# A two-layer decoder trunk on one core: the up projections' matmuls sorted by width, and low parts moved 64 bytes

## The chip, the cores and the metric

The kernel runs on one core of a Trainium2 chip. The metric is the device time of one execution in microseconds (us); three runs of the kernel before have a median of 771.84 (771.66 to 772.72). TensorE (PE) multiplies, VectorE (DVE) and ScalarE (ACT) do elementwise work, GpSimd (POOL) a few small steps, and SyncE's queue (SP) issues the transfers from main memory (HBM) to the on-chip memory (SBUF). Matmul results land in PSUM. A matmul has a *stationary* operand, which a weight load (LDWEIGHTS, PEld in the profile) brings into the array, and a *moving* one, which streams past it, one column of the result per column of the operand.

## The reference

The input x is 256 tokens by 1024 features, float32. Layer 0 mixes tokens by dilated attention (three patterns, 16 heads of 64), layer 1 by forgetting attention; a dense feed-forward layer follows each, and a final norm ends it.

```python
def swiglu(h, w_gu, w_down):
    gu = h @ w_gu
    g, u = gu[..., :D_FF], gu[..., D_FF:]
    return (jax.nn.silu(g) * u) @ w_down

for i in range(DEPTH):                         # DEPTH = 2
    h = h + mixer[i](rmsnorm(h, norm[i]))      # projections, attention, output projection
    h = h + swiglu(rmsnorm(h, ffn_norm[i]), ffn_w_gu[i], ffn_w_down[i])   # D_FF = 2816
return rmsnorm(h, final_norm)
```

All inputs are float32, and every weight is read once from HBM.

## The kernel before

**Three-part products.** A float32 matrix is split into a high part, rounded to the format `float32r` that TensorE streams in one pass, and a low part, the remainder. `split` (L73, L74) does this: ScalarE copies into the high tile, VectorE subtracts it from the source into the low tile. A product is then the sum of high x high, high x low and low x high, three matmuls into one PSUM bank: `mm3` (L172, L173, L174).

**Weights.** `piece` fetches a weight piece of 128 x 2048 in two halves into `raw` tiles (5 buffers of 4 KB per partition) and splits each half into `wh` and `wl` (4 buffers of 8 KB each). `weights` keeps two pieces ahead in a fixed order of pieces.

**x^T.** `xt_tile` holds the normalised activations transposed: for each of 8 depths k (128 features each) 256 columns of the high part and behind them 256 of the low part, in one tile of 16 KB per partition with one buffer. It is used by every projection of a mixer and of a feed-forward layer.

**Projections.** `proj_feat` takes weights as stationary operand and x^T as moving one (256 columns, feature-major result); `proj_tok` and `proj_pair` take x^T as stationary operand and weights as moving one (256 and 512 columns, token-major result). `out_proj` and `down` take attention outputs (`oth`, `otl`) or activations (`ah`, `al`) as stationary operand and 512 columns of weights as moving one.

**The up projection, `proj_wide`.** For 19 of the 22 pieces of each feed-forward layer, once for the gate and once for the up half, it goes through the 8 depths. At each depth one matmul (L224) has the high weights stationary and streams high and low of x^T together, 512 columns into the whole bank; the next (L225) has the low weights stationary and streams the high part, 256 columns into the bank's first half. Widths thus alternate 512, 256, 512, 256. Behind it ScalarE and VectorE add the bank's halves, and apply the gate. The first three pieces of each feed-forward layer (its head) run through `proj_tok` instead, while the second half of the tokens is still being normalised.

**What sets the order.** All of it is written in program order, and a planner places each engine's instructions by that order and by a priority (`first()` lifts the few that shorten a chain). The last up projection of each feed-forward layer is lifted whole, so it interleaves with the one before it.

**Where tiles lie.** Three pools stand one behind the other in SBUF: `cst`, `wp` (weights) and `ap` (all else). In a pool, the first use of a name reserves all its buffers at the next free address, each rounded up to 32 bytes. `p_tile` gives a tile of 768 floats, which serves attention weights and, with 512 floats used, the high and low activations `ah` and `al` of the feed-forward layers. A tile of 112 floats (448 bytes) that nothing reads stands ahead of x^T. Small tiles for norms and softmax (`rs`, `ssq`, `nm`, `den`, `gates`, `rs_a`, `rt`) lie where their first use comes.

Of the kernel before, what the change touches and what calls it, by code (L numbers as in the profile page):

```python
# [10 lines left out]
F32 = mybir.dt.float32  # L11
F32R = mybir.dt.float32r
# [4 lines left out]
P = 128  # L17
D = 1024
S = 256
KT = D // P  # L20
NH = 16
# [10 lines left out]
def trunk(ctx: ExitStack, tc: tile.TileContext, T, out):  # L32
    nc = tc.nc

    cst = ctx.enter_context(tc.tile_pool(name="cst", bufs=1))
    wp = ctx.enter_context(tc.tile_pool(name="wp", bufs=1))
    ap = ctx.enter_context(tc.tile_pool(name="ap", bufs=1))
    ps = ctx.enter_context(tc.tile_pool(name="ps", bufs=1, space=bass.MemoryType.PSUM))

    ALL = slice(None)  # L40
# [8 lines left out]
    def hrow(name):  # L49
        return ap.tile([P, D], F32, tag="h", name=name, bufs=4)  # L50
# [16 lines left out]
    euler = cst.tile([P, 1], F32, name="euler")  # L67
    nc.gpsimd.memset(euler, math.e)

    def split(pair, view, src, early=True):  # L70
        hi, lo = pair
        with first() if early else nullcontext():
            return (nc.scalar.activation(view(hi), src, AF.Copy),  # L73
                    nc.vector.tensor_tensor(view(lo), src, view(hi).bitcast(F32), op=ALU.subtract))  # L74
# [18 lines left out]
    def fm_tile(tag, n, bufs):  # L93
        return tuple(ap.tile([P, n, S], F32R, tag=f"{tag}{x}", name=f"{tag}{x}", bufs=bufs) for x in "hl")
# [1 line left out]
    class XT(tuple):  # L96
        pass

    def xt_tile():
        full = ap.tile([P, KT, 2, S], F32R, tag="xt", name="xt", bufs=1)  # L100
        x = XT((full[:, :, 0, :], full[:, :, 1, :]))
        x.full = full
        return x
# [72 lines left out]
    def both(pair, *idx):  # L176
        return tuple(x[idx] for x in pair)
# [41 lines left out]

    def proj_wide(xt, w, o, c):  # L220

        for k in range(KT):
            wh, wl = both(w, ALL, slice(k * 256 + c * P, k * 256 + (c + 1) * P))
            nc.tensor.matmul(o.rearrange("p (x s) -> p x s", x=2), wh, xt.full[:, k], start=k == 0, stop=False)  # L224
            nc.tensor.matmul(o[:, :S], wl, xt[0][:, k], start=False, stop=k == KT - 1)  # L225


    def p_tile(n=512, dtype=F32, name="p"):
        return ap.tile([P, 768], dtype, tag="p", name=name, bufs=6)[:, :n]

    def v_tile(o=None, r=None):

# [57 lines left out]
    o = psum("o")  # L290
    for n in (256, 256, 256, 256, 128):
        nc.tensor.matmul(o[:, :n], mhalf.to_broadcast([P, P]), mhalf.to_broadcast([P, n]), start=True, stop=True)
    with tc.high_priority(offset=1000):
# [1 line left out]

    room = [hrow("xw0"), hrow("xw1"), *(y.rearrange("p k c -> p (k c)").bitcast(F32) for y in fm_tile("ot", KT, 1)),
            wp.tile([P, 2048], F32, tag="wh", name="xw4", bufs=4)]
    xk, wk, xs = [], [], []  # L300
    for i, c in enumerate(room):
        b = 1 + (i > 1)
        n = S + 512
# [12 lines left out]
        for j in range(b):  # L316
            xk.append(both_k[:, j, :S])
            wk.append(both_k[:, j, S:])

    ap.tile([P, 112], F32, tag="gap", name="gap", bufs=1)  # L320
    xt = xt_tile()

    r_a = []
    lead = [psum("sc") for _ in range(2)]
# [49 lines left out]
    with first(), in_order(cut):  # L374
        a = square(4)
# [11 lines left out]
    def rstd_a():  # L387

        o = psum("tr")
        for t in range(2):  # L390
            nc.tensor.matmul(o[:, t:t + 1], part[0][:, t * P:(t + 1) * P], one, start=True, stop=True)
        v = ap.tile([P, 4], F32, tag="rs_a", name="rs_a", bufs=1)
        with first():
            nc.scalar.activation(v[:, :2], o[:, :2], AF.Copy, bias=EPS)
            nc.gpsimd.tensor_tensor(v[:, 2:], v[:, :2], mhalf.to_broadcast([P, 2]), op=ALU.pow)
        r_a.extend(v[:, 2 + t:3 + t] for t in range(2))

    x = []
# [101 lines left out]
    for i, (hq, g, w) in enumerate(a_units):  # L500
# [18 lines left out]
        if w < 2:  # L519
# [4 lines left out]
            if i == 2:  # L524
                values_12(quad["v"], lead)

                wt = weights("a_in", 1)
                o_next = psum("mm")
                rb = psum("tr")

                def rows():
                    for t in range(2):
                        nc.tensor.matmul(rb[:, t * P:(t + 1) * P], r_a[t].to_broadcast([P, P]), ident,
                                         start=True, stop=True)

                proj_feat(xt, wt, o_next[:, :S], 0, (6, rows))
                for c in (rcos, rsin):
                    nc.vector.tensor_tensor(c, c, rb[:, :S], op=ALU.mult)
                rt = ap.tile([P, 2], F32, tag="rt", name="rt", bufs=1)
                tmp = ap.tile([P, D], F32, tag="xn", name="rd", bufs=2)[:, :S].rearrange("p (b c) -> p b c", b=2)  # L540
                e = early(rb[:, :S], None)
                nc.vector.tensor_tensor(tmp, e, ident[:, None, :].to_broadcast([P, 2, P]), op=ALU.mult)
                nc.vector.tensor_reduce(rt, tmp, axis=AX.X, op=ALU.add)
# [65 lines left out]
    def out_proj(nm, ot, h, grow, done, banks):  # L609

        ws = [weights(nm, i) for i in range(4)]
        xt = xt_tile()
        res = []

        def part(t, acc, nk):
# [36 lines left out]
    def ffn(l, hs, xt, grow, mid):  # L652
        acc = {}
        acts = {}

        def act(f):
            if f % 2 == 0:
                acts[f // 2] = tuple(p_tile(512, F32R, f"a{y}") for y in "hl")
            return acts[f // 2], lambda y: y[:, (f % 2) * S:(f % 2 + 1) * S]

        def gated(g, u, shape):
# [94 lines left out]

    def mid(h0):
        nxt["g"] = load_grow(2)
        nxt["xt"] = xt_tile()
        norm_t(*h0, nxt["g"], nxt["xt"], 0)  # L760

    hs = ffn(0, hs, xt, g_f, mid)
# [6 lines left out]
    split((wf[:, :, :NH], wf[:, :, 32:32 + NH]), lambda y: y, wf32.rearrange("p (k c) -> p k c", k=KT))  # L769

    gt = v_tile()
    ga = ap.tile([P, 6, 2 * NH], F32, tag="gates", name="gates", bufs=1)


    own = (slice(0, 64), slice(64, 128))
# [286 lines left out]
```

## Time and profile before

| | |
|---|---|
| median of 3 runs | 771.84 us (771.66 to 772.72) |
| the profiled execution's own time | 772.96 us |
| its span | 771.1 us |
| granted TensorE clock, mean | 0.996 of full |
| PE busy | 760.3 us (99%) |
| weight loads busy | 675.2 us (88%) |
| DVE busy | 535.7 us (69%) |
| ACT busy | 429.9 us (56%) |
| HBM read | 133.05 MB, 174 GB/s over the span |

A row of the groups reads: line, engine, operation, out<-in by the program's names, partitions x columns, count | busy us, mean ns of one | idle time of the engine just before them, and what ended it. For a matmul, `128*128 128x512` is a stationary operand of 128 x 128 and a moving one of 128 x 512. Matmuls are pipelined: their recorded durations overlap, so the time that one costs in a stream is the difference between its start and the next one's. A timeline row begins with the start and the duration in us.

### The profile page before, as it was taken

The page shows a single profiled execution, that of the slowest core. Times are in us where ns is not written, and L with a number is a line of the kernel's source. Part 1 is how long each engine was busy: PE and PEld are TensorE (multiplying, and loading weights), DVE is VectorE, ACT ScalarE, POOL GpSimd, SP SyncE. Part 2 cuts the span into 40 slices and gives each one's busy share as a digit, 9 for nine tenths or more (in the row PEclk, how much of TensorE's full clock was granted, in tenths as well). Part 3 has the DMA queues.
Part 4 walks back from the last instruction along what each step waited for, and adds up shares of the span by engine and source line. Part 5 has one row for each costly group of instructions (what it writes and reads, how often), then busy time and mean ns, then how long its engine had stood idle before and what let it go on. Part 6 is the DMA issues. An engine that isn't in the chain of part 4 may idle for free.

```text
span 771.1 us, 12961 instructions
## 1 busy us (share of the span) xinstructions
PE 760.3 (99%) x5152; PEld 675.2 (88%) x5152; DVE 535.7 (69%) x834; ACT 429.9 (56%) x740; POOL 33.4 (4%) x51
## 2 busy tenths in 40 slices
PE   9999999999999999999999999999999999999996
PEld 7988999999998798888888888999889888888885
DVE  7897986976988476665566474887756656567644
ACT  7735628448538455545565464586655455556532
POOL 1110000010010000000000003110000000000000
PEclk9999999999999999999999999999999999999999
DMA  9864561752663367555567544643326655656601
GB/s 330 291 198 158 164 213 63 236 176 88 206 215 118 98 217 242 185 192 190 180 199 232 153 148 153 217 139 122 119 89 228 214 195 183 192 190 196 213 1 54
DMA packets 38348, 134.93 MB, mean 175 GB/s; under 512 B 4368, under 2 KB 5648, under 8 KB 38288
## 3 DMA queue, kind: packets, MB, share of 16 engines
q1 hardware_dynamic: 38144, 134.01, 52.6%
q8 instruction: 40, 0.66, 0.3%
q14 instruction: 20, 0.16, 0.1%
q10 hardware_dynamic: 144, 0.10, 0.0%
HBM read 133.05 MB, written 1.05 MB: 174 GB/s over the span
## 4 chain that ended last, share of the span: by engine, by line
PE 86%; DVE 5%; ACT 3%; DMA 2%; issue 2%; POOL 1%; SPq 0%; POOLq 0%; DVEq 0%; ACTq 0%
PE ps_mm L172 10%; PE ps_mm L174 10%; PE ps_mm L173 10%; PE ps_tr L224 9%; PE ps_mm L224 9%; PE ps_mm L225 5%; PE ps_tr L225 5%; PE ps_sc L174 4%; PE ps_sc L172 4%; PE ps_sc L173 4%; PE ps_o L174 3%; PE ps_o L173 3%; PE ps_o L172 3%; PE ps_tr L272 2%; PE ps_o L283 2%
## 5 line engine op out<-in xcount | busy, mean ns | idle before, releaser
L74 DVE TENSOR_TENSOR wl<-raw,wh 128x1024 fp32r<-128x1024 f32 x236 | 284.0, 1219 | 146.3 <-ACT wh L73 146.0
L73 ACT ACTIVATE wh<-raw 128x1024 fp32r<-128x1024 f32 x236 | 243.7, 1056 | 154.2 <-PE ps_tr L224 34.8
L172 PE MATMUL ps_mm<-xt,wh 128*128 128x256 f32 x512 | 144.1, 281 | 0.0
L174 PE MATMUL ps_mm<-xt,wl 128*128 128x256 f32 x512 | 142.3, 278 | 0.1
L173 PE MATMUL ps_mm<-xt,wh 128*128 128x256 f32 x512 | 142.1, 278 | 0.0
L224 PE MATMUL ps_tr<-xt,wh 128*128 128x512 f32 x304 | 108.8, 397 | 0.0
L224 PE MATMUL ps_mm<-xt,wh 128*128 128x512 f32 x304 | 108.7, 397 | 0.0
L174 PEld LDWEIGHTS ps_mm<-xt,wl 128*128 128x128 f32 x512 | 96.5, 188 | 0.5 <-DVE wl L74 0.5
L172 PEld LDWEIGHTS ps_mm<-xt,wh 128*128 128x128 f32 x512 | 96.2, 188 | 0.4
L173 PEld LDWEIGHTS ps_mm<-xt,wh 128*128 128x128 f32 x512 | 96.4, 188 | 0.2
L225 PE MATMUL ps_mm<-xt,wl 128*128 128x256 f32 x304 | 85.1, 281 | 0.0
L225 PE MATMUL ps_tr<-xt,wl 128*128 128x256 f32 x304 | 85.1, 281 | 0.0
L224 PEld LDWEIGHTS ps_tr<-xt,wh 128*128 128x128 f32 x304 | 57.0, 188 | 13.9
L224 PEld LDWEIGHTS ps_mm<-xt,wh 128*128 128x128 f32 x304 | 57.0, 188 | 13.6
L172 PE MATMUL ps_mm<-wh,xt 128*128 128x256 f32 (+1 forms) x176 | 60.2, 342 | 2.0 <-DVE fm L409 2.0
L173 PE MATMUL ps_mm<-wl,xt 128*128 128x256 f32 (+1 forms) x176 | 59.1, 336 | 0.0
L174 PE MATMUL ps_mm<-wh,xt 128*128 128x256 f32 (+1 forms) x176 | 59.0, 336 | 0.0
L225 PEld LDWEIGHTS ps_mm<-xt,wl 128*128 128x128 f32 x304 | 57.1, 188 | 0.9
L225 PEld LDWEIGHTS ps_tr<-xt,wl 128*128 128x128 f32 x304 | 57.1, 188 | 0.2
L73 ACT ACTIVATE ah<-sa 128x256 fp32r<-128x256 f32 x38 | 15.9, 418 | 49.5 <-DVE sa L684 49.5
L172 PEld LDWEIGHTS ps_mm<-wh,xt 128*128 128x128 f32 x176 | 33.9, 193 | 6.1 <-issue 2.4
L174 PEld LDWEIGHTS ps_mm<-wh,xt 128*128 128x128 f32 x176 | 33.8, 192 | 3.7 <-DVE xt L74 0.3
(243 smaller groups left out, 1263.3 us busy)
## 6 DMA issues: line engine op xcount, KB each, us to landing
raw<-in_gu SPq DMA_DIRECT2D x88, 512.0 KB, 4.7
raw<-in_a_in SPq DMA_DIRECT2D x68, 512.0 KB, 4.6
raw<-in_dn SPq DMA_DIRECT2D x44, 512.0 KB, 4.7
raw<-in_b_in SPq DMA_DIRECT2D x24, 512.0 KB, 4.9
raw<-in_a_out SPq DMA_DIRECT2D x8, 512.0 KB, 4.0
raw<-in_b_out SPq DMA_DIRECT2D x8, 512.0 KB, 4.2
grow<-in_norms SPq DMA_DIRECT2D x4, 512.0 KB, 5.9
x<-in_x SPq DMA_DIRECT2D x2, 512.0 KB, 5.4
```

Source lines behind the costliest of these rows:

```text
L73: return (nc.scalar.activation(view(hi), src, AF.Copy), nc.vector.tensor_tensor(view(lo), src, view(hi).bitcast(F32), op=ALU.subtract))
L74: nc.vector.tensor_tensor(view(lo), src, view(hi).bitcast(F32), op=ALU.subtract))
L172: nc.tensor.matmul(o, sh, mh, start=start, stop=False)
L173: nc.tensor.matmul(o, sh, ml, start=False, stop=False)
L174: return nc.tensor.matmul(o, sl, mh, start=False, stop=stop)
L224: nc.tensor.matmul(o.rearrange("p (x s) -> p x s", x=2), wh, xt.full[:, k], start=k == 0, stop=False)
L225: nc.tensor.matmul(o[:, :S], wl, xt[0][:, k], start=False, stop=k == KT - 1)
L272: nc.tensor.transpose(tr[:, i * P:(i + 1) * P], b, ident)
L283: nc.tensor.matmul(o[h * HD:(h + 1) * HD], v[:, c:c + HD], w(h), start=start, stop=stop)
```

## The change

Three things change; the arithmetic stays.

- `proj_wide` runs its 8 matmuls of 512 columns first and then its 8 of 256.
- A tile of 16 floats (64 bytes) stands between the buffers of `wh` and those of `wl`, so the low weights lie 64 bytes further from the high ones than a whole number of 512 bytes. The low part of the activations starts 16 floats into its tile (`at`).
- `xt_tile` has two forms. With `gap` (the mixers) the high and the low half are separate blocks, 16 floats apart; without (the feed-forward layers) they alternate by depth as before, 16 floats from the tile's start. The attention outputs `otl` and `oth` are reserved in two places, and the small tiles are reserved earlier (`small`, `place`), so that their sizes set the addresses of the others; the 112-float tile is gone.

```diff
-    def xt_tile():
-        full = ap.tile([P, KT, 2, S], F32R, tag="xt", name="xt", bufs=1)
+    def xt_tile(gap):
+
+        tile = ap.tile([P, 2, KT * S + 16], F32R, tag="xt", name="xt", bufs=1)
+        if gap:
+            full = tile[:, :, :KT * S].rearrange("p x (k s) -> p k x s", k=KT)
+        else:
+            n = KT * S * 2
+            full = tile.rearrange("p x n -> p (x n)")[:, 16:16 + n].rearrange("p (k x s) -> p k x s", k=KT, x=2)
...
     def proj_wide(xt, w, o, c):
 
+        wh, wl = ([y[:, k * 256 + c * P:k * 256 + (c + 1) * P] for k in range(KT)] for y in w)
         for k in range(KT):
-            wh, wl = both(w, ALL, slice(k * 256 + c * P, k * 256 + (c + 1) * P))
-            nc.tensor.matmul(o.rearrange("p (x s) -> p x s", x=2), wh, xt.full[:, k], start=k == 0, stop=False)
-            nc.tensor.matmul(o[:, :S], wl, xt[0][:, k], start=False, stop=k == KT - 1)
+            nc.tensor.matmul(o.rearrange("p (x s) -> p x s", x=2), wh[k], xt.full[:, k], start=k == 0, stop=False)
+        for k in range(KT):
+            nc.tensor.matmul(o[:, :S], wl[k], xt[0][:, k], start=False, stop=k == KT - 1)
...
-    def p_tile(n=512, dtype=F32, name="p"):
-        return ap.tile([P, 768], dtype, tag="p", name=name, bufs=6)[:, :n]
+    def p_tile(n=512, dtype=F32, name="p", at=0):
+        return ap.tile([P, 768], dtype, tag="p", name=name, bufs=6)[:, at:at + n]
...
-    room = [hrow("xw0"), hrow("xw1"), *(y.rearrange("p k c -> p (k c)").bitcast(F32) for y in fm_tile("ot", KT, 1)),
+    room = [hrow("xw0"), hrow("xw1"), None, ap.tile([P, KT, S], F32R, tag="otl", name="otl", bufs=1),
             wp.tile([P, 2048], F32, tag="wh", name="xw4", bufs=4)]
+    wp.tile([P, 16], F32, tag="gap", name="gap", bufs=1)
+    small["gates"] = ap.tile([P, 6, 2 * NH], F32, tag="gates", name="gates", bufs=1)
+    place("rs", 2, 4)
+    xt = xt_tile(64)
+    place("ssq", 1, 8)
+    place("nm", 4, 3)
+    place("den", 4, 3)
+    room[2] = ap.tile([P, KT, S], F32R, tag="oth", name="oth", bufs=1)
+    room[2:4] = (y.rearrange("p k c -> p (k c)").bitcast(F32) for y in room[2:4])
...
-    ap.tile([P, 112], F32, tag="gap", name="gap", bufs=1)
-    xt = xt_tile()
...
-        xt = xt_tile()
+        xt = xt_tile(0)
...
-                acts[f // 2] = tuple(p_tile(512, F32R, f"a{y}") for y in "hl")
+                acts[f // 2] = p_tile(512, F32R, "ah"), p_tile(512, F32R, "al", 16)
...
-        nxt["xt"] = xt_tile()
+        nxt["xt"] = xt_tile(64)
```

Here `small` holds `rs_a` and `rt`, now reserved in the pool `cst`, and `place(tag, n, bufs)` reserves the named small tile.

More of the change, by code (lines that the diff above doesn't have):

```diff
@@ L68, in trunk, with place @@
     nc.gpsimd.memset(euler, math.e)
+    small = {y: cst.tile([P, n], F32, name=y) for y, n in (("rs_a", 4), ("rt", 2))}
+    def place(tag, n, bufs):
+        ap.tile([P, n], F32, tag=tag, name=tag, bufs=bufs)
     def split(pair, view, src, early=True):
@@ L391, in rstd_a @@
             nc.tensor.matmul(o[:, t:t + 1], part[0][:, t * P:(t + 1) * P], one, start=True, stop=True)
-        v = ap.tile([P, 4], F32, tag="rs_a", name="rs_a", bufs=1)
+        v = small["rs_a"]
         with first():
@@ L538, in trunk @@
                     nc.vector.tensor_tensor(c, c, rb[:, :S], op=ALU.mult)
-                rt = ap.tile([P, 2], F32, tag="rt", name="rt", bufs=1)
+                rt = small["rt"]
                 tmp = ap.tile([P, D], F32, tag="xn", name="rd", bufs=2)[:, :S].rearrange("p (b c) -> p b c", b=2)
@@ L771, in trunk @@
     gt = v_tile()
-    ga = ap.tile([P, 6, 2 * NH], F32, tag="gates", name="gates", bufs=1)
+    ga = small["gates"]
     own = (slice(0, 64), slice(64, 128))
```

## The prediction

> **What bounds the kernel now.** I read the page's busy shares first, then the chain of waits, then the groups by line, then the timeline of TensorE in each kind of stage.
>
> ```profile
> span 771.1 us, 12961 instructions
> PE 760.3 (99%) x5152; PEld 675.2 (88%) x5152; DVE 535.7 (69%) x834; ACT 429.9 (56%) x740; POOL 33.4 (4%) x51
> PEclk9999999999999999999999999999999999999999
> PE 86%; DVE 5%; ACT 3%; DMA 2%; issue 2%; POOL 1%; SPq 0%; POOLq 0%; DVEq 0%; ACTq 0%
> L224 PE MATMUL ps_tr<-xt,wh 128*128 128x512 f32 x304 | 108.8, 397 | 0.0
> L224 PE MATMUL ps_mm<-xt,wh 128*128 128x512 f32 x304 | 108.7, 397 | 0.0
> L225 PE MATMUL ps_mm<-xt,wl 128*128 128x256 f32 x304 | 85.1, 281 | 0.0
> L225 PE MATMUL ps_tr<-xt,wl 128*128 128x256 f32 x304 | 85.1, 281 | 0.0
> ```
>
> TensorE is busy all the way, its clock is granted throughout, and 86% of the chain that ended last is its work. The lines to be reordered, L224 and L225, ran 608 times each (304 + 304), with 0.0 us of idle time ahead of them: nothing is late there, and only the time from one matmul's start to the next one's (I call it the step) can change. Busy times overlap, so steps are taken from the timeline. Here is the end of one pass of the up projection (8 depths) and the down projection behind it:
>
> ```profile
> 305.19 0.40 PE L224 MATMUL ps_tr<-xt,wh 128*128 128x512 f32 x1
> 305.43 0.28 PE L225 MATMUL ps_tr<-xt,wl 128*128 128x256 f32 x1
> 305.55 0.40 PE L224 MATMUL ps_tr<-xt,wh 128*128 128x512 f32 x1
> ...
> 308.02 0.39 PE L172 MATMUL ps_sc<-wh,ah 128*128 128x512 f32 x1
> ...
> 309.87 0.39 PE L174 MATMUL ps_sc<-wh,al 128*128 128x512 f32 x1
> ...
> 313.49 0.39 PE L224 MATMUL ps_mm<-xt,wh 128*128 128x512 f32 x1
> ```
>
> One pass, 305.19 to 308.02, takes 2.83 us: 0.354 us for a pair, 0.24 for its 512 columns and 0.12 for its 256. 76 passes (608 / 8) are 215 us, 28% of the span. The down projection has the same 512 columns. Its first eight matmuls behind the up projection (308.02 to 309.87) take 0.231 us each, the next sixteen (309.87 to 313.49) 0.2263. So a 512-column matmul in a settled row of its like is about 9 ns faster than one between 256s. In the groups the recorded mean is the step plus some 163 ns (0.2263 goes with 0.39).
>
> What else steps differ by is seen in the stages that have one width alone:
>
> ```profile
> 81.15 0.28 PE L172 MATMUL ps_mm<-xt,wh 128*128 128x256 f32 x1
> ...
> 83.87 0.28 PE L172 MATMUL ps_mm<-xt,wh 128*128 128x256 f32 x1
> ```
> ```profile
> 183.33 0.28 PE L172 MATMUL ps_mm<-xt,wh 128*128 128x256 f32 x1
> ...
> 186.16 0.28 PE L172 MATMUL ps_mm<-xt,wh 128*128 128x256 f32 x1
> ```
> ```profile
> 272.35 0.28 PE L172 MATMUL ps_o<-wh,xt 128*128 128x256 f32 x1
> ...
> 275.18 0.28 PE L172 MATMUL ps_o<-wh,xt 128*128 128x256 f32 x1
> ```
> ```profile
> 762.24 0.28 PE L172 MATMUL ps_mm<-wh,ah 128*128 128x256 f32 x1
> ...
> 763.55 0.28 PE L174 MATMUL ps_tr<-wh,al 128*128 128x256 f32 x1
> ```
> ```profile
> 177.84 0.39 PE L172 MATMUL ps_mm<-wh,xt 128*128 128x512 f32 x1
> ...
> 180.59 0.39 PE L172 MATMUL ps_mm<-wh,xt 128*128 128x512 f32 x1
> ```
>
> The first two fences are the same projection, 24 matmuls of 256 columns, at 2.72 us and at 2.83: 0.1133 or 0.1179 each. So the same code settles in one of two rhythms. The token-wise projection has 0.1179 (24 in 2.83), the last 256s of the kernel 0.1191 (11 in 1.31), and the 512-column projection with x^T as stationary operand 0.2292 (12 in 2.75).
>
> **Addresses.** All weight tiles, and everything ahead of x^T, are whole multiples of 512 bytes long; the gap tile of 112 floats (448 bytes) puts x^T 7 x 64 bytes off that grid. Behind x^T the tiles rs_a and rt, 32 bytes each, bring the rest back onto it. So x^T lies an odd number of 64-byte lines from the weights, while activations (ah, al) and attention outputs (oth, otl) lie a whole number of 512 bytes from them; I say "apart" and "even". By the rows above: 512 columns even 0.2263, apart 0.2292; 256 columns even 0.1191, apart 0.1133 or 0.1179. Wide matmuls do better even, narrow ones apart. That is few rows, and a reading of mine: no row holds all else equal.
>
> The diff gives the up projection just that pairing. By its tile sizes x^T of the feed-forward layers (gap 0, 16 floats in) comes to lie even with wh, read against it in the 512s, and apart from wl, read in the 256s, because the new 16-float gap tile moves all wl by 64 bytes. Elsewhere high goes with high and low with low (x^T of the attention layers, oth/otl, ah/al), so those distances stay as they are.
>
> **The change part by part.**
>
> *The order in the up projection.* Nothing is added: per pass 8 matmuls of 512, then 8 of 256, same operands and same bank. Eight 512s cost between 8 x 0.2263 = 1.810 us (settled) and 1.85 (the eight behind 308.02, which also follow 256s). I take 1.85, since every new row of 512s follows a row of 256s. Eight 256s cost between 8 x 0.1133 = 0.907 and 8 x 0.1191 = 0.953. I take 0.907, from the row that has the same moving tensor, the same kind of stationary one and the same distance. Sum 2.757 against 2.83: 0.073 us a pass, times 76 = **5.5 us gained**, with ends of 0.113 x 76 = 8.6 and 0.027 x 76 = 2.1.
>
> *Distances in the heads of the feed-forward layers.* Their first three pieces are token-wise, with x^T stationary: 3 x 2 x 8 x 3 matmuls in each of 2 layers are 288. Here high x low now lies apart, but the two with the high weights lie even. Bounds: from 0.1179 to 0.1191, a loss of 0.35 us, and to 0.1133, a gain of 1.3. I take **0.3 us lost**, by the even 256s of the kernel's end.
>
> *High and low 64 bytes apart in all other three-part products.* Distances stay, but each product now steps to the other 64-byte line and back. The trace has no such alternation. Below, nothing, or a gain where all 256s settle at 0.1133: their mean is that of the first three rows here:
>
> ```profile
> L172 PE MATMUL ps_mm<-xt,wh 128*128 128x256 f32 x512 | 144.1, 281 | 0.0
> L174 PE MATMUL ps_mm<-xt,wl 128*128 128x256 f32 x512 | 142.3, 278 | 0.1
> L173 PE MATMUL ps_mm<-xt,wh 128*128 128x256 f32 x512 | 142.1, 278 | 0.0
> L172 PE MATMUL ps_o<-wh,ah 128*128 128x512 f32 x78 | 30.4, 390 | 0.0
> L172 PE MATMUL ps_sc<-wh,ah 128*128 128x512 f32 x80 | 31.5, 394 | 0.0
> L172 PE MATMUL ps_sc<-oth,ah 128*128 128x512 f32 x8 | 3.1, 393 | 0.0
> L172 PE MATMUL ps_o<-oth,ah 128*128 128x512 f32 x8 | 3.1, 389 | 0.0
> L172 PE MATMUL ps_sc<-wh,oth 128*128 128x512 f32 x32 | 13.0, 407 | 0.0
> L172 PE MATMUL ps_mm<-wh,oth 128*128 128x512 f32 x32 | 13.0, 407 | 0.0
> ```
>
> It is 279, or a step of 0.116, so 1536 x 0.003 = 4 us at the very most, about half of it waits rather than rhythm: 2 us. Above, the price is the second rival's (the other five rows count its calls). I take nothing, because in every row here the step goes with the distance and the kind of neighbour, and those are kept.
>
> *Low weights are needed later.* wl is now first read 1.8 us into a pass. This gains nothing, since L225 never waited. The splits stay covered, from 308 to 436 us:
>
> ```profile
> L74 DVE TENSOR_TENSOR wl<-raw,wh 128x1024 fp32r<-128x1024 f32 x45 | 54.3, 1221 | 45.2 <-ACT wh L73 45.2
> L73 ACT ACTIVATE wh<-raw 128x1024 fp32r<-128x1024 f32 x46 | 47.9, 1055 | 22.7 <-PE ps_tr L224 15.5 <-PE ps_o L174 7.1
> ```
>
> In these 128 us VectorE idled 45 us and ScalarE 23 ahead of them; a TensorE that is 2% faster takes some 2.6 us of that. If that cover were gone, a late split would cost at most its 1.22 us, once a piece.
>
> *Small tiles and their places.* rs_a, rt, gates, rs, ssq, nm and den are only allocated elsewhere: no instruction, no transfer and no buffer count changes, so nothing.
>
> The sum is 5.5 - 0.3 = 5.2 us. The profiled execution has a span of 771.1 and a time of 772.96, 1.1 above the median of the runs, 771.84. I take the gain off each alike: a span of 765.9 and a median of **766.6 us**.
>
> **A rule that speaks against it.** The Trainium skill (TensorE: Matmul & The Clock Gate, Step-by-step: what each phase is for) says that the array reads the moving operand and the next weights through two independent ports, so that loading weights takes nothing from the running matmul; by that rule neither order nor address matters and the time stays at 771.8. The trace does not agree: 512 columns step by 0.2263 in one place and by 0.24 in another with no wait in either.
>
> **The rivals.**
>
> 1. *The steps do not hang on order or distance* but on the operands themselves: x^T moving costs 0.235 whatever stands beside it. For it: no row of the trace has x^T moving in a row of 512s with full weights. Against it: x^T moving in 256s reaches 0.1133, below the 0.12 that it has here. Time 771.8, or 771 to 772.6.
>
> 2. *Slower: alternating lines keep the three-part products from settling.* The down projection needs eight matmuls to settle when it comes from other operands (0.231 against 0.2263). If each switch between high and low starts that anew, 714 wide matmuls (down and output projections: 80 + 78 + 8 + 8 + 32 + 32 calls of three) lose 0.0047 each, 3.4 us, and the 1536 narrow ones go from their mean 0.116 to 0.1191, 4.8 us. Together 8.2 lost against 5.2 gained: 774.8. It decides from a loss of 2.3 ns over these 2250 matmuls. For it: two rhythms of one code show that neighbours matter. Against it: a step of 0.2263 holds over all three products in turn today.
>
> 3. *Everything settles at once.* Each row of 512s runs at 0.2263 from its first matmul, which gains 8.6 us, and the 256s elsewhere all fall to 0.1133, 2 us more: 771.84 - 10.6 + 0.3 = 761.5. For it: the down projection's second half needs no settling; against it: its first eight do.
>
> 4. *The narrow rows fall into the slower rhythm*, and the gain is 2.1 to 3.4 us: 768.4 to 769.7. For it: each 256 stage that follows 512s without a pause (183.33, 272.35) runs at 0.1179. This is inside the forecast's own bounds.
>
> **How the numbers follow.** Forecast with the fourth case, 764 to 770: 0.54. Third, 759.5 to 764: 0.20. First: 0.13. Second: 0.13. A measurement of this kernel can tell about 0.2% (1.5 us) from no change. Faster: 0.54 + 0.20 = 0.74; same 0.13; slower 0.13. The range runs from 760.5, cutting the tail of the third case, to 772.5, taking in no change but leaving out the second.
>
> **What would show it.** In the changed profile the two groups of the 512s in the up projection should have a mean near 0.231 + 0.163 = 394 ns or less (397 now) and the 256s 276 (281 now); a pass should take 2.76 us. The down groups should keep 390 to 394 and the 256s of the attention projections 278 to 281: higher means that the second rival holds. If the up groups still show 397 and 281, the first one does. I am wrong if the idle time ahead of L224's successors is no longer 0, or if the gain stands at lines that the order does not touch.

## The result, and the profile after

The changed kernel takes **774.52 us** (median of 12 runs, 773.54 to 775.6) against 772.72 for the kernel before, timed beside it. The ratio is 1.0023, with a 95% interval of 1.0014 to 1.0032: slower, by a hair more than the 0.2% that I had called the bound of what can be told. One of the twelve runs of the kernel before took 1070.4 us and is left out of the ratio; the median is the same without it. The forecast was 766.6, and 774.52 lies outside its range, on the second rival's side.

The page of the changed kernel, first its head, busy shares and granted clock, then the chain of waits by engine:

```profile
span 772.8 us, 12962 instructions
PE 763.0 (99%) x5152; PEld 679.3 (88%) x5152; DVE 539.7 (70%) x834; ACT 430.8 (56%) x740; POOL 32.7 (4%) x51
PEclk9999999999999999999999999999999999999999
PE 88%; DVE 4%; ACT 3%; issue 2%; DMA 2%; SPq 0%; POOL 0%; POOLq 0%; DVEq 0%; ACTq 0%
```

The span grew by 1.7 us (771.1 before). The matmuls are as many as before (5152) and the granted clock is nearly the same (0.998, before 0.996), but TensorE is busy 2.7 us longer and has 88% of the chain, not 86%. Nothing else became a bound: the loss is inside the matmuls' steps.

The groups of the changed kernel, in the form of those shown of before. `mm3` is now L186 to L188, and `proj_wide` L238 and L240:

```profile
L186 PE MATMUL ps_mm<-xt,wh 128*128 128x256 f32 x512 | 146.4, 286 | 0.0
L188 PE MATMUL ps_mm<-xt,wl 128*128 128x256 f32 x512 | 144.1, 281 | 0.0
L187 PE MATMUL ps_mm<-xt,wh 128*128 128x256 f32 x512 | 143.9, 281 | 0.0
L238 PE MATMUL ps_tr<-xt,wh 128*128 128x512 f32 x304 | 76.0, 392 | 0.0
L238 PE MATMUL ps_mm<-xt,wh 128*128 128x512 f32 x304 | 75.7, 391 | 0.0
L240 PE MATMUL ps_mm<-xt,wl 128*128 128x256 f32 x304 | 42.0, 281 | 0.0
L186 PE MATMUL ps_o<-wh,ah 128*128 128x512 f32 x78 | 30.9, 396 | 0.0
L187 PE MATMUL ps_o<-wl,ah 128*128 128x512 f32 x78 | 30.7, 394 | 0.0
L186 PE MATMUL ps_sc<-wh,oth 128*128 128x512 f32 x32 | 13.2, 412 | 0.0
```

Read the means, not the busy times: matmuls of one line now follow each other, and their overlapping records are merged in the sum. The up projection's 512s fell from 397 to 391.5 ns, its 256s stayed at 281. The three feature-major groups of the attention projections rose from 281, 278 and 278 to 286, 281 and 281, and the down projection's from 390 and 389 to 396 and 394. No row has idle time ahead of it. So part of the gain came where I looked for it, and more was lost at lines whose order did not change.

In the timeline of the changed kernel, here is one pass of the up projection up to the down projection's first matmul, and 24 matmuls of a feature-major projection:

```profile
308.31 2.00 PE L238 MATMUL ps_tr<-xt,wh 128*128 128x512 f32 x8
310.14 1.11 PE L240 MATMUL ps_tr<-xt,wl 128*128 128x256 f32 x8
311.09 0.39 PE L186 MATMUL ps_sc<-wh,ah 128*128 128x512 f32 x1
```
```profile
72.22 0.28 PE L186 MATMUL ps_mm<-xt,wh 128*128 128x256 f32 x1
72.33 0.28 PE L187 MATMUL ps_mm<-xt,wh 128*128 128x256 f32 x1
72.45 0.28 PE L188 MATMUL ps_mm<-xt,wl 128*128 128x256 f32 x1
72.56 0.29 PE L186 MATMUL ps_mm<-xt,wh 128*128 128x256 f32 x1
72.69 0.28 PE L187 MATMUL ps_mm<-xt,wh 128*128 128x256 f32 x1
...
75.06 0.28 PE L186 MATMUL ps_mm<-xt,wh 128*128 128x256 f32 x1
```

A pass takes 1.83 us for its 512s (0.229 each) and 0.95 for its 256s (0.119 each), 2.78 us in all: 0.05 less than before, not the 0.073 that I had forecast. The feature-major products no longer run evenly. The five quoted starts are 0.11, 0.12, 0.11 and 0.13 us apart, and 24 steps take 2.84 us (0.1183 each) where the faster rhythm of before took 2.72.

One small gain was not foreseen: the longest wait of TensorE, before and after.

```profile
PE ps_mm L172 <- DVE fm L409: 2.0, 1, 2.0
```
```profile
PE ps_mm L186 <- DVE fm L430: 0.8, 1, 0.8
```

For the account I took every step (start to next start) of the trace and summed them by stage. Totals hold all steps; a mean leaves out those over 1.25 times the stage's median, which I take for waits. The clock alone (0.996 before, 0.998 after) could make a row 0.2% shorter, 0.4 us in the largest.

| stage | count | before, us (ns each) | after, us (ns each) | difference, us |
|---|---|---|---|---|
| feature-major 256s | 1536 | 180.0 (114.7) | 185.3 (118.6) | +5.3 |
| down projection | 522 | 119.5 (228.1) | 120.8 (230.5) | +1.3 |
| output projection | 192 | 45.5 (228.3) | 46.0 (231.4) | +0.5 |
| heads' token-wise 256s | 288 | 34.8 (117.6) | 35.1 (118.4) | +0.2 |
| attention's token-wise 256s | 192 | 24.0 (118.9) | 23.9 (118.9) | 0.0 |
| up projection, 512s | 608 | 142.7 (234.7) | 139.4 (229.2) | -3.3 |
| up projection, 256s | 608 | 72.0 (118.4) | 71.6 (117.8) | -0.4 |
| 512s with x^T stationary, waits included | 288 | 71.8 (229.8) | 70.1 (231.5) | -1.7 |

That is 7.3 us lost and 5.4 gained, or 1.9 us net; the span says 1.7. The last row mixes two things: its steps grew by 1.7 ns, some 0.5 us in all, and its waits shrank by about 2.1. The attention's token-wise 256s, whose low parts moved as well, lost nothing.

### The profile page after: what moved, and what is told of

Its sections match the earlier page's. It is cut to its first block, busy times and chain, and to the rows that moved or that the text cites. A ratio compares the mean times of both kernels' runs of the same rounds, so it can differ in the third digit from the quotient of the medians.

```text
span 772.8 us, 12962 instructions
## 1 busy us (share of the span) xinstructions
PE 763.0 (99%) x5152; PEld 679.3 (88%) x5152; DVE 539.7 (70%) x834; ACT 430.8 (56%) x740; POOL 32.7 (4%) x51
## 4 chain that ended last, share of the span: by engine, by line
PE 88%; DVE 4%; ACT 3%; issue 2%; DMA 2%; SPq 0%; POOL 0%; POOLq 0%; DVEq 0%; ACTq 0%
PE ps_mm L186 11%; PE ps_mm L188 11%; PE ps_mm L187 11%; PE ps_tr L238 9%; PE ps_mm L238 9%; PE ps_tr L240 5%; PE ps_mm L240 5%; PE ps_sc L186 4%; PE ps_sc L188 4%; PE ps_sc L187 4%; PE ps_o L186 3%; PE ps_o L187 3%; PE ps_o L188 3%; PE ps_tr L287 2%; PE ps_o L298 2%
## 5 line engine op out<-in xcount | busy, mean ns | idle before, releaser
L81 ACT ACTIVATE wh<-raw 128x1024 fp32r<-128x1024 f32 x236 | 240.3, 1055 | 147.2 <-PE ps_mm L187 41.7
L186 PE MATMUL ps_mm<-xt,wh 128*128 128x256 f32 x512 | 146.4, 286 | 0.0
L188 PE MATMUL ps_mm<-xt,wl 128*128 128x256 f32 x512 | 144.1, 281 | 0.0
L187 PE MATMUL ps_mm<-xt,wh 128*128 128x256 f32 x512 | 143.9, 281 | 0.0
L186 PEld LDWEIGHTS ps_mm<-xt,wh 128*128 128x128 f32 x512 | 96.9, 189 | 0.4
L187 PEld LDWEIGHTS ps_mm<-xt,wh 128*128 128x128 f32 x512 | 97.0, 189 | 0.2
L188 PEld LDWEIGHTS ps_mm<-xt,wl 128*128 128x128 f32 x512 | 96.3, 188 | 0.4 <-DVE wl L82 0.4
L238 PE MATMUL ps_tr<-xt,wh 128*128 128x512 f32 x304 | 76.0, 392 | 0.0
L238 PE MATMUL ps_mm<-xt,wh 128*128 128x512 f32 x304 | 75.7, 391 | 0.0
L238 PEld LDWEIGHTS ps_mm<-xt,wh 128*128 128x128 f32 x304 | 55.7, 188 | 11.1
L238 PEld LDWEIGHTS ps_tr<-xt,wh 128*128 128x128 f32 x304 | 54.4, 188 | 9.8
L186 PE MATMUL ps_mm<-wh,xt 128*128 128x256 f32 (+1 forms) x176 | 59.7, 339 | 0.8 <-DVE fm L430 0.8
L187 PE MATMUL ps_mm<-wl,xt 128*128 128x256 f32 (+1 forms) x176 | 58.7, 333 | 0.0
L188 PE MATMUL ps_mm<-wh,xt 128*128 128x256 f32 (+1 forms) x176 | 58.5, 333 | 0.0
L240 PEld LDWEIGHTS ps_mm<-xt,wl 128*128 128x128 f32 x304 | 41.3, 189 | 2.9
L240 PEld LDWEIGHTS ps_tr<-xt,wl 128*128 128x128 f32 x304 | 41.3, 189 | 2.9
L240 PE MATMUL ps_tr<-xt,wl 128*128 128x256 f32 x304 | 42.0, 281 | 0.0
L240 PE MATMUL ps_mm<-xt,wl 128*128 128x256 f32 x304 | 42.0, 281 | 0.0
L186 PEld LDWEIGHTS ps_mm<-wh,xt 128*128 128x128 f32 x176 | 33.4, 190 | 4.8 <-issue 1.2
L701 ACT ACTIVATE low<-ps_mm 128x256 f32<-128x256 f32 x38 | 14.6, 385 | 40.8 <-PE ps_mm L240 40.8
```

Source lines behind the costliest of these rows:

```text
L81: return (nc.scalar.activation(view(hi), src, AF.Copy), nc.vector.tensor_tensor(view(lo), src, view(hi).bitcast(F32), op=ALU.subtract))
L186: nc.tensor.matmul(o, sh, mh, start=start, stop=False)
L187: nc.tensor.matmul(o, sh, ml, start=False, stop=False)
L188: return nc.tensor.matmul(o, sl, mh, start=False, stop=stop)
L238: nc.tensor.matmul(o.rearrange("p (x s) -> p x s", x=2), wh[k], xt.full[:, k], start=k == 0, stop=False)
L240: nc.tensor.matmul(o[:, :S], wl[k], xt[0][:, k], start=False, stop=k == KT - 1)
```

## The experiments

The question was which of the two, order or addresses, makes the gain, which makes the loss, and what it is about an address that does it. The expectations name their theories by letters, and each says there what it holds (D is narrowed between the kernels with 128 and with 256 bytes). Differences are against the kernel before, run beside the experiment on the same chip. Where no interval is given, it is one run of each.

**The order alone.** The kernel before, with only the order of `proj_wide` changed:

```diff
+        wh, wl = ([y[:, k * 256 + c * P:k * 256 + (c + 1) * P] for k in range(KT)] for y in w)
         for k in range(KT):
-            wh, wl = both(w, ALL, slice(k * 256 + c * P, k * 256 + (c + 1) * P))
-            nc.tensor.matmul(o.rearrange("p (x s) -> p x s", x=2), wh, xt.full[:, k], start=k == 0, stop=False)
-            nc.tensor.matmul(o[:, :S], wl, xt[0][:, k], start=False, stop=k == KT - 1)
+            nc.tensor.matmul(o.rearrange("p (x s) -> p x s", x=2), wh[k], xt.full[:, k], start=k == 0, stop=False)
+        for k in range(KT):
+            nc.tensor.matmul(o[:, :S], wl[k], xt[0][:, k], start=False, stop=k == KT - 1)
```

> The kernel before with the new order of the up projection alone; no address moves. Theory A (the order gains, stepping between odd and even 64-byte lines loses): three-part products keep the steps of before (down 0.2263 us, attention projections 0.1133 to 0.1179), a pass of the up projection falls from 2.83 us to about 2.78 (8 x 0.2292 + 8 x 0.1179), 76 x 0.05 = 3.8 us: some 769 against 772.7. Theory B (the order itself gains nothing, the changed kernel's gain in the up projection comes from the distances): a pass stays at 2.83, 772.7. Theory C (the order costs elsewhere, in the planner's placing): slower than 772.7 with the down groups above 390 ns.

768.92 us against 772.44; ratio 0.9950 (0.9936 to 0.9964). The groups of this kernel (`proj_wide` is L224 and L226, `mm3` starts at L172) and a pass in its timeline:

```profile
L172 PE MATMUL ps_mm<-xt,wh 128*128 128x256 f32 x512 | 144.1, 281 | 0.0
L224 PE MATMUL ps_mm<-xt,wh 128*128 128x512 f32 x304 | 77.0, 394 | 0.0
L226 PE MATMUL ps_mm<-xt,wl 128*128 128x256 f32 x304 | 41.0, 277 | 0.0
L172 PE MATMUL ps_o<-wh,ah 128*128 128x512 f32 x78 | 30.4, 390 | 0.0
```
```profile
303.49 2.02 PE L224 MATMUL ps_mm<-xt,wh 128*128 128x512 f32 x8
305.36 1.07 PE L226 MATMUL ps_mm<-xt,wl 128*128 128x256 f32 x8
306.27 0.39 PE L224 MATMUL ps_tr<-xt,wh 128*128 128x512 f32 x1
```

The order is worth 3.5 us, as theory A had it, and all else stays as before (281 and 390). Here the 256s do what I had forecast (0.91 us for eight), and the 512s gain less (1.87 us, 394 ns).

**The addresses alone.** The changed kernel with the old alternating loop:

```diff
-        wh, wl = ([y[:, k * 256 + c * P:k * 256 + (c + 1) * P] for k in range(KT)] for y in w)
         for k in range(KT):
-            nc.tensor.matmul(o.rearrange("p (x s) -> p x s", x=2), wh[k], xt.full[:, k], start=k == 0, stop=False)
-        for k in range(KT):
-            nc.tensor.matmul(o[:, :S], wl[k], xt[0][:, k], start=False, stop=k == KT - 1)
+            wh, wl = both(w, ALL, slice(k * 256 + c * P, k * 256 + (c + 1) * P))
+            nc.tensor.matmul(o.rearrange("p (x s) -> p x s", x=2), wh, xt.full[:, k], start=k == 0, stop=False)
+            nc.tensor.matmul(o[:, :S], wl, xt[0][:, k], start=False, stop=k == KT - 1)
```

> The changed kernel with the old order of the up projection (512, 256, 512, 256): addresses alone. Theory A: the loss of the three-part products alone, some 1.8 us measured plus 3.6 that the order no longer gives back: 777 to 779, down groups 391 to 396 ns, attention projections 281 to 286. Theory B: the up projection keeps a part of its gain by distance: below 776. Theory C: 772.7 or less.

774.34 us against 772.44, ratio 1.0024 (1.0015 to 1.0034). That is theory B's side; A had 777 to 779. Its groups (`proj_wide` is L238 and L239):

```profile
L186 PE MATMUL ps_mm<-xt,wh 128*128 128x256 f32 x512 | 146.5, 286 | 0.0
L238 PE MATMUL ps_tr<-xt,wh 128*128 128x512 f32 x304 | 107.0, 392 | 0.0
L239 PE MATMUL ps_tr<-xt,wl 128*128 128x256 f32 x304 | 84.7, 280 | 0.0
L186 PE MATMUL ps_o<-wh,ah 128*128 128x512 f32 x78 | 30.9, 396 | 0.0
```

The whole loss is in the addresses (286 and 396). And so is a gain in the up projection: 392 and 280 ns with the old order, within 1 ns of the new. By steps, order alone gains 3.5 us in the up projection, addresses alone 3.7, both together 3.7. **The two do not add up:** at the new addresses the order is worth nothing that can be measured (774.52 against 774.34, ratios 1.0023 and 1.0024).

**Twice the displacement.** The changed kernel with 128 bytes in place of 64, small tiles re-placed so that the high parts keep their distances. The low weights move with the rest, so the 256s of the up projection come to lie 128 bytes from x^T, modulo 256, where they lay 192:

```diff
-        tile = ap.tile([P, 2, KT * S + 16], F32R, tag="xt", name="xt", bufs=1)
+        tile = ap.tile([P, 2, KT * S + 32], F32R, tag="xt", name="xt", bufs=1)
...
-    wp.tile([P, 16], F32, tag="gap", name="gap", bufs=1)
+    wp.tile([P, 32], F32, tag="gap", name="gap", bufs=1)
...
-                acts[f // 2] = p_tile(512, F32R, "ah"), p_tile(512, F32R, "al", 16)
+                acts[f // 2] = p_tile(512, F32R, "ah"), p_tile(512, F32R, "al", 32)
```

> The changed kernel with high and low 128 bytes apart in place of 64 (weights, mixers' x^T, attention outputs, activations); the feed-forward x^T stays even with the high weights; new order. Theory A (what costs is the step from an even 64-byte line to an odd one and back): at 128 bytes every operand begins on a line of the same parity as its partner, three-part products settle again, down groups at 389 to 391 ns and attention projections at 276 to 281; the 256s of the up projection are now even and run at 0.119: 769 to 771. Theory D (any displacement of low against high costs): as the changed kernel, 774 to 775, down groups 391 to 396.

779.7 us, ratio 1.0095 (1.0082 to 1.0108), the slowest of all. Its groups and, in its timeline, twelve matmuls of the down projection:

```profile
L187 PE MATMUL ps_mm<-xt,wh 128*128 128x256 f32 x512 | 146.6, 286 | 0.0
L188 PE MATMUL ps_mm<-xt,wl 128*128 128x256 f32 x512 | 145.2, 284 | 0.0
L187 PE MATMUL ps_o<-wl,ah 128*128 128x512 f32 x78 | 30.9, 396 | 0.0
```
```profile
312.46 0.39 PE L186 MATMUL ps_sc<-wh,ah 128*128 128x512 f32 x1
...
315.24 0.39 PE L186 MATMUL ps_o<-wh,ah 128*128 128x512 f32 x1
```

Twelve take 2.78 us (0.2317 each; 0.2263 settled). Were it a matter of stepping between odd and even 64-byte lines (theory A), 128 bytes would have cured it. It made it worse: 120.7 ns in the feature-major stages against 118.6, which is 3.3 of the 5 us; another 1.5 are in the up projection's 256s (120.3 ns against 117.8). The other theory, 774 to 775, was passed as well.

**Four times the displacement.** 256 bytes in all three places (against the changed kernel); for this the gates' eight 512-column matmuls became sixteen of 256, and small tiles were re-placed to keep the distances:

```diff
-    wp.tile([P, 16], F32, tag="gap", name="gap", bufs=1)
+    wp.tile([P, 64], F32, tag="gap", name="gap", bufs=1)
...
+            x = XT(tile[:, y:y + n].rearrange("p (k s) -> p k s", k=KT) for y in (0, n + 64))
...
-                acts[f // 2] = p_tile(512, F32R, "ah"), p_tile(512, F32R, "al", 16)
+                acts[f // 2] = p_tile(512, F32R, "ah"), p_tile(512, F32R, "al", 64)
```

> As the changed kernel, but high and low parts 256 bytes apart (weights, mixers' x^T, attention outputs, activations); feed-forward x^T even with the high weights; the gates' eight wide matmuls are sixteen of 256. Theory D (three-part products settle only where an operand's start repeats, modulo some length, from one matmul to the next): if that length is 256 bytes or less, down groups fall back to 389 to 391 ns and attention projections to 276 to 280, 769 to 771; if it is 512 or more they stay at 391 to 396 and 281 to 287, 774 to 780. Rival E (the cost grows with the displacement, 64 to 128 bytes gave 2 to 7 us more than before): above 780.

769.55 us against 771.53. The groups (`mm3` is L187 to L189), and 24 feature-major matmuls in the timeline:

```profile
L187 PE MATMUL ps_mm<-xt,wh 128*128 128x256 f32 x512 | 143.8, 281 | 0.0
L188 PE MATMUL ps_mm<-xt,wh 128*128 128x256 f32 x512 | 141.9, 277 | 0.0
L187 PE MATMUL ps_o<-wh,ah 128*128 128x512 f32 x78 | 30.4, 390 | 0.0
```
```profile
72.15 0.28 PE L187 MATMUL ps_mm<-xt,wh 128*128 128x256 f32 x1
...
74.87 0.28 PE L187 MATMUL ps_mm<-xt,wh 128*128 128x256 f32 x1
```

24 steps in 2.72 us, 0.1133 each: everything that 64 and 128 bytes had unsettled is settled again (114.3 ns feature-major, 227.9 in the down projection). A cost that grows with the displacement (theory E) is out. Of the theories named, D is left: these products settle where an operand's start repeats, from one matmul to the next, modulo some length. 64 and 128 bytes break it, 256 doesn't, so the length is 256 bytes, as far as these three sizes tell. There is a rival, the distance between the operands of one matmul. `mm3` multiplies high by high, high by low and low by high, so with 64 or 128 bytes two of its three matmuls have their two operands at a new distance from each other, and with 256 all three have the old one, modulo 256. A start that repeats and a distance that is kept come and go together in these three kernels.

**One side alone.** Two kernels with the old order. In the first `al` and the low half of the mixers' x^T are 64 bytes further and the weights are not (here too the gates' eight wide matmuls are sixteen of 256); in the second the low weights alone are. Small tiles are re-placed in both, which is not shown:

```diff
-                acts[f // 2] = tuple(p_tile(512, F32R, f"a{y}") for y in "hl")
+                acts[f // 2] = p_tile(512, F32R, "ah"), p_tile(512, F32R, "al", 16)
...
+            x = XT(tile[:, y:y + n].rearrange("p (k s) -> p k s", k=KT) for y in (0, n + gap))
```

> The kernel before (old order) with two low parts moved 64 bytes and the weights left: the activations' (stationary in the down projection, the weights moving do not step) and the mixers' x^T (moving in the feature-major projections, whose stationary weights do not step; stationary in the token-major ones). Theory D, both sides count: down groups 391 to 396 in place of 389 to 390, feature-major projections 281 to 286 in place of 278 to 281. If only the moving side counts: down stays at 389 to 391, feature-major rises. If only the stationary side counts: the reverse. Distances change too in the third of the products with a low part, so under the distance reading alone a third of the down matmuls goes from 0.2263 to 0.2292: mean 390 to 391.

```diff
+    wp.tile([P, 16], F32, tag="gap", name="gap", bufs=1)
+    small["gates"] = ap.tile([P, 6, 2 * NH], F32, tag="gates", name="gates", bufs=1)
+    place("rs", 2, 4)
+    xt = xt_tile(64)
...
```

> The kernel before (old order) with the low weights alone moved 64 bytes: the moving side steps in the down, output and token-major projections, the stationary side in the feature-major ones. Both sides count: down 391 to 396, output and feature-major groups up as well, 774 or more less what the up projection gains by distance (its 256s now lie even). Only the moving side: down and output up, feature-major as before (278 to 281). Only the stationary side: feature-major up to 281 to 286, down stays at 389 to 391.

775.76 and 777.57 us, against 771.53. The groups of the first, then of the second (`mm3` is L180 to L182, and L181 to L183):

```profile
L180 PE MATMUL ps_mm<-xt,wh 128*128 128x256 f32 x512 | 145.8, 285 | 0.0
L180 PE MATMUL ps_o<-wh,ah 128*128 128x512 f32 x78 | 30.4, 390 | 0.0
L181 PE MATMUL ps_o<-wl,ah 128*128 128x512 f32 x78 | 30.6, 392 | 0.0
L182 PE MATMUL ps_o<-wh,al 128*128 128x512 f32 x78 | 31.0, 397 | 0.0
```
```profile
L181 PE MATMUL ps_mm<-xt,wh 128*128 128x256 f32 x512 | 146.5, 286 | 0.0
L181 PE MATMUL ps_o<-wh,ah 128*128 128x512 f32 x78 | 30.8, 395 | 0.0
L183 PE MATMUL ps_o<-wh,al 128*128 128x512 f32 x78 | 30.8, 395 | 0.0
```

In the first kernel the displaced operand is the stationary one of the down projection and the moving one of the feature-major stages; in the second it is the other way about. Both stages are unsettled in both (118.0 and 231.4 ns; 118.2 and 231.6). So displacing the low part of either operand is enough. The output projection, whose operands the first leaves in place, kept 228.4 ns there and has 231.9 in the second. That is the control within the run. The rows of the down projection speak for both readings: in the first kernel the loss is mostly in the product whose own distance changed (397; the other two 390 and 392, a mean of 393 where the expectation had 390 to 391 for distance alone), in the second the product of the two high parts, which both stayed, loses as much as the others (395, before 390). So a new distance inside a matmul can't be all; what lies ahead of it or behind it counts too.

**The order with x^T placed by itself.** No displacement between high and low, the new order, and the feed-forward x^T moved within its tile: onto the weights' grid (0 bytes), 64 bytes off it, 128 bytes off it. The first diff is against the kernel before, the other two against the first; some small tiles move so that the rest stays. In the kernel with the order alone it is 448 bytes off, which is 192 modulo 256.

```diff
+    small = {y: cst.tile([P, n], F32, name=y) for y, n in (("rs_a", 4), ("rt", 2))}
...
+        tile = ap.tile([P, n + 16], F32R, tag="xt", name="xt", bufs=1)
+        full = tile[:, at:at + n].rearrange("p (k x s) -> p k x s", k=KT, x=2)
...
-        xt = xt_tile()
+        xt = xt_tile(16)
```

> The kernel before with the new order and the feed-forward x^T moved by 64 bytes so that it lies even with both weight parts; high and low are not moved apart. By the distance reading (512 columns settle at 0.2263 even, 0.2292 apart; 256 columns 0.119 even, 0.1133 to 0.118 apart) the 512s of a pass take 1.83 us and its 256s 0.955, the heads of the feed-forward layers go from 0.1179 to 0.119: a pass of 2.785, 769 to 770, a little slower than the order alone or equal to it. If distance to x^T does not matter at all: the same groups as with the order alone.

```diff
-        tile = ap.tile([P, n + 16], F32R, tag="xt", name="xt", bufs=1)
+        tile = ap.tile([P, n + 80], F32R, tag="xt", name="xt", bufs=1)
...
-        xt = xt_tile(16)
+        xt = xt_tile(32)
```

> New order, high and low parts not moved apart, feed-forward x^T 64 bytes from the weights' grid (weights' grid minus 64 for the weight loads of the up projection, plus 64 for the loads of x^T in the heads). Theory F (what counts is how far, modulo 256 bytes, the next weight load lies from the operand that is streaming: 0, 64, 128 and 192 each have their own rhythm): heads go to 0.1133 as the feature-major projections do at plus 64 (means 276 in place of 281), up projection like the token-wise ones at 192: 512s 0.229 to 0.233, 256s 0.118, a pass of 2.78 to 2.81; 767.5 to 770. The reading of the prediction (even against odd lines): all groups as with the order alone, heads 281, 512s 395, 256s 277; 769.

```diff
-        xt = xt_tile(16)
+        xt = xt_tile(48)
```

> As the order with an even x^T, but the feed-forward x^T 128 bytes from the weights' grid in place of 0. Even against odd (the reading of the prediction): the same groups as at 0, 512s of the up projection near 392 ns, 256s near 282, heads 283. If the distance itself counts, other means; if distance does not count, the groups of the order alone (512s 395 to 396, 256s 277).

| x^T to weights, modulo 256 | time, us | kernel before, us; ratio | up 512s, ns | up 256s, ns |
|---|---|---|---|---|
| 192 (order alone) | 768.92 | 772.44; 0.9950 (0.9936 to 0.9964) | 232.9 | 114.4 |
| 0 | 769.59 | 772.44; 0.9969 (0.9957 to 0.9980) | 229.3 | 119.1 |
| 64 | 767.5 | 771.78; 0.9945 (0.9931 to 0.9959) | 229.7 | 116.8 |
| 128 | 772.44 | 771.53 | 232.5 | 118.6 |

The groups of the up projection (L228, L230) at 64 bytes, then at 128:

```profile
L228 PE MATMUL ps_mm<-xt,wh 128*128 128x512 f32 x304 | 76.1, 392 | 0.0
L230 PE MATMUL ps_tr<-xt,wl 128*128 128x256 f32 x304 | 42.0, 280 | 0.0
L230 PE MATMUL ps_mm<-xt,wl 128*128 128x256 f32 x304 | 41.4, 278 | 0.0
```
```profile
L228 PE MATMUL ps_mm<-xt,wh 128*128 128x512 f32 x304 | 77.0, 395 | 0.0
L230 PE MATMUL ps_mm<-xt,wl 128*128 128x256 f32 x304 | 42.4, 282 | 0.0
```

A pair costs 347 to 351 ns in all four, against 353 in the alternating order, and no place is good for both widths. At 0 bytes the distance reading had it right: 229 and 119 ns, heads at 119.9, 769.59 us where it said 769 to 770. But "even" and "apart" cannot be all there is: 64 and 192 bytes are both odd numbers of 64-byte lines and differ by 3 ns in the 512s, 0 and 128 both even numbers of lines and differ by 3 as well. (The granted clock was 0.995 in the traces of 192 and 128 bytes, 0.999 and 0.998 in those of 0 and 64; that is 0.9 ns of the 3.) Theory F took each distance modulo 256 to have a rhythm of its own. The four places do differ, but it had the heads' 256s at 113.3 ns at 64 bytes, where they measured 117.7. The kernel at 64 bytes is the fastest of the study and beats both kernels; its lead over the order alone is within what the two intervals leave open.

The table also gives a price, as an estimate, to the distance inside a matmul as the cause of the loss, since its 256s have weights stationary and x^T moving as the feature-major ones do. Before, all three products of a feature-major projection have 192 bytes; in the changed kernel they have 192, 0 and 128, with 128 bytes of displacement 192, 64 and 64. By distance alone that makes (114.4 + 119.1 + 118.6) / 3 = 117.4 ns, where 118.6 were measured, and (114.4 + 116.8 + 116.8) / 3 = 116.0, where 120.7 were. So distance inside a matmul may well be a good part of the loss, but it would make 128 bytes the better spacing, and 128 was the worse. No run moves the starts and keeps all distances, so how the rest is shared stays open.

**Longer rows.** The order alone, but 16 matmuls of 512 (gate and up) and then 16 of 256:

```diff
...
+        for c, o in enumerate(os):
+            for k in range(KT):
+                nc.tensor.matmul(o.rearrange("p (x s) -> p x s", x=2), part(0, c, k), xt.full[:, k], start=k == 0, stop=False)
+        for c, o in enumerate(os):
+            for k in range(KT):
+                nc.tensor.matmul(o[:, :S], part(1, c, k), xt[0][:, k], start=False, stop=k == KT - 1)
```

> The order alone, carried further: sixteen matmuls of 512 (both halves of a piece), then sixteen of 256; addresses as before. If a change of width costs a few unsettled matmuls and nothing else, half of these changes go: 7 to 10 ns for each of 38 halves, 0.3 to 0.6 us below the order alone (768.3 to 768.6). If what sets the 512s at 0.233 is the distance, their mean stays at 395 to 396 however long the row, and the time equals the order alone within what can be measured. Slower than the order alone would mean that the later gate half is waited for.

769.22 us against 771.78; 0.9964 (0.9950 to 0.9977). Its groups:

```profile
L226 PE MATMUL ps_tr<-xt,wh 128*128 128x512 f32 x304 | 77.0, 395 | 0.0
L229 PE MATMUL ps_tr<-xt,wl 128*128 128x256 f32 x304 | 40.7, 276 | 0.0
```

Half as many changes of width gain nothing: 233.2 and 114.2 ns against 232.9 and 114.4. At this distance the 512s stay near 233 in a long row too, so it is not the width change ahead of them that keeps them there; their place does, by the 229.3 and 229.7 ns at 0 and 64 bytes.

## Why the prediction was wrong

- **What bounds the kernel: right.** TensorE is busy throughout, and but for the early wait only its steps changed, at nearly the same clock.
- **The step that failed** is "*High and low 64 bytes apart in all other three-part products*", which I took at "nothing, because in every row here the step goes with the distance and the kind of neighbour, and those are kept". It cost 7.1 us (5.3 + 1.3 + 0.5). The distances are not kept. I wrote that "high goes with high and low with low", but only one product in three has two parts of a kind; in high x low and low x high one operand moved by 64 bytes and the other didn't. I had seen this for the heads and not here. By my own "even" and "apart", 476 of the 714 wide matmuls would have gone from 0.2263 to 0.2292 and 1024 of the 1536 narrow ones from 0.116 to 0.1191: 1.4 + 3.2 = 4.6 us lost, and a forecast of 771.2. What the runs show in its place: with 64 or 128 bytes between high and low the products run unsettled, with 256 they settle, and moving the low part on one side is enough. Whether it is the new distances or the starts that change from one matmul to the next, or both, they don't show.
- **The second rival** named the loss, by alternating lines that keep the products from settling. Its price was right in sum (8.2 us; 7.1 measured) and off in its parts: 3.4 for the wide ones (1.8 measured), 4.8 for the narrow ones (5.3). Its time, 774.8, is 0.3 from the median, which is partly luck: it set 8.2 us against a gain of 5.2 and counted from 771.84, where the trace has 7.3 against 5.4 and the kernel before took 772.72 beside it. I gave it 0.13, because the trace had no such alternation and "a step of 0.2263 holds over all three products in turn today" seemed to speak against it. It didn't: those products started on one grid, all at one distance.
- **The order in the up projection** was mis-sized: 5.5 us forecast, 3.7 measured. The 512s came in at 0.229, a little better than the 0.231 that I took. The 256s came in at 0.1178, not 0.1133; this is the fourth rival's slower rhythm, also inside the forecast's bounds. I had taken 0.1133 "from the row that has the same moving tensor, the same kind of stationary one and the same distance". In the order alone, at that distance, they do reach 0.1144; in the changed kernel, at that same distance but behind 512s at another one, they don't. So the distance alone doesn't set the rhythm. That it is how the row is entered is my reading, and no run isolates it.
- **Why it gained** was wrong as well. I priced it as order, and distance as what helps the order. By the two halves of the change either does it by itself, and the second adds nothing. The 512s step by 229 to 230 ns wherever x^T lies even with the high weights, in rows (229.3) or alternating (229.9).
- **The reading "even" and "apart"** had too few rows, as the prediction said. The four places of x^T show that it is too coarse: the place counts, but not by odd and even lines alone.
- **Heads, low weights needed later, small tiles:** 0.2 us lost (0.3 forecast) in the heads; no idle time at L240 from the later reading of the low weights. The early stage of 512s with x^T stationary took 1.7 us less, by shorter waits, which I did not foresee. Its longest wait, 2.0 us before, was 2.0 with the order alone and 0.6 with the addresses alone, so it goes with the new places; which of them was not tried.
- **The Trainium skill's rule** (TensorE: Matmul & The Clock Gate, Step-by-step: what each phase is for), by which the next weights come in through a port of their own and take nothing from the running matmul, would, as I read it, have made the changed kernel and the one with 128 bytes, which run the same matmuls in the same order, equal but for their waits. They took 774.52 and 779.7 us; I was right not to follow it, and wrong to think that this left no room for a loss by addresses.

## What to carry to other kernels

When a change claims a gain at one place by moving buffers, price every other matmul that reads those buffers: 2250 matmuls at 2 to 4 ns each undid what 1216 had gained. Write down for each of them which two tiles it reads: where low parts alone move, every product of a high and a low part changes its distance. Keep the high and low parts of an operand a multiple of 256 bytes apart, the one spacing tried above zero that kept these rows settled, and try order and address as separate changes, since the one can already hold the gain of the other. Where TensorE shows no idle time and the clock is full, compare the mean of one matmul by group and shape; the shares say nothing of this.

## What the hardware showed that I had not expected

The same instructions in the same order, with 0.0 us of idle time ahead of these groups, differ by 5 us with the place of their operands: 774.52 us with 64 bytes between high and low, 779.7 with 128. A displacement counts modulo 256 bytes as far as 64, 128 and 256 tell. In the down projection it costs about as much on the stationary side as on the moving one (231.4 and 231.6 ns, 228.1 before). Stages that ran in the faster rhythm lost it (feature-major, 114.7 to 118.6 ns); the attention's token-wise 256s, at 118.9 before, stayed there. A stage of one width has more than one rhythm (0.1133 or about 0.118 us for 256 columns, 0.2263 or 0.229 to 0.233 for 512).

What in the hardware has this period stays open: the traces show starts, and not what a start waits for. Not tried were starts that change while every distance is kept, displacements between 128 and 256 bytes, one of 512, and the fastest kernel with other places for the rest of its tiles.
